# A decoder block on one core: GpSimd adds up one probability tile in four, ScalarE takes some of VectorE's copies, key splits are spread

## The chip, the cores and the metric

The kernel runs on one core of a Trainium2 chip. The metric is the device time of one execution in microseconds; it is the median over runs.

The engines are called as the profile calls them: PE (TensorE, the matrix engine; PEld is its weight loading), DVE (VectorE), ACT (ScalarE), POOL (GpSimd), SP (SyncE, which here only issues transfers).

## What is computed

One layer of a decoder block over 2048 positions with 1024 channels. The change touches attention alone. It has three groups of eight heads of 64 channels; each group looks at keys with a stride (1, 4, 16), in blocks of 128 queries against the block before and the own block:

```python
s = jnp.einsum('brnqhd,brnkhd->brnhqk', qb, kw) * (Dh ** -0.5)
s = jnp.where(valid[None, None, :, None], s, NEG_INF)
m = jnp.max(s, axis=-1, keepdims=True)
p = jnp.exp(s - m)
l = jnp.sum(p, axis=-1, keepdims=True)
o = jnp.einsum('brnhqk,brnkhd->brnqhd', p, vw)
```

Later `o / l` of the three groups are mixed with weights from `m + log(l)`. So each row of `p` needs its sum `l`, but nothing in attention itself waits for `l`: it is stored, and read after attention.

## The kernel before

The kernel has three stages. The input projection (up to 1443.7 us of the profiled span) is a long row of matrix products. Attention follows, to about 1645 us. Then come the output products.

Attention is written as 48 rounds, `i` from 0 to 47 (counted from 0 throughout this text; "rounds 9 to 40" of the change's short description, counted from 1, are `i` = 8 to 39). Four rounds make a unit: one group and one pair of heads. The groups take turns: rounds 0 to 3 are of group 0, 4 to 7 of group 2, 8 to 11 of group 1, 12 to 15 of group 0 again. A round has four query blocks `j`, each with two heads `h`. Where a block has no block of keys before it (all of group 2, the first round of a unit of group 1, one block in the first round of a unit of group 0) its rows are 128 wide, else 256. Twelve rounds (24 to 35, say) are one full turn of the pattern.

The order of the instructions on each engine is the order of the code; nothing moves them. In round `i` the code does this:

- `scores(i)`: PE makes the scores in four PSUM tiles (`s`), 24 products.
- `peak(i, j, h)`: DVE adds the mask, writes the tile `p` and takes the row's extreme into `sta` (L1015).
- `expo(i, j, h)`: ACT takes the exponential of `p` in place; with `accum_out` it also sums each row into `sta` (L1023). The sum is fetched by an instruction of its own, ACTIVATION_READ_ACCUMULATOR.
- `turn(i-1, w)`: PE transposes the pair `w` of tiles `p` of the round before into PSUM (`pt`, L1034).
- `bring(i, w, k, eng)`: DVE (L1049) or ACT (L1047) copies one half of that to SBUF (`ptb`).
- `values(i-2)`: PE multiplies with the values into `o` (L1064), and `leave(i-3)` copies `o` out on DVE (L1073 to L1079).

Three of the four copies of a round have fixed engines. The fourth, `bring(i-2, 1, 0, ...)`, goes to DVE when `light` holds, else to ACT.

A tile `p` lives in a pool of eight buffers, so the tile of round `i` is written again by `peak` of round `i+2`.

POOL splits each unit's keys into a high and a low part, in four quarters, each a CAST (L809) and a TENSOR_TENSOR (L811) on the tile `B` of the unit. The keys of unit `u` are loaded in round `4u-8` and used from round `4u` on. `later(lag, fn)` puts `fn` at the start of the round that is `lag` rounds on.

Of the kernel before, what the change touches and what calls it, by code (L numbers as in the profile page):

```python
# [8 lines left out]
F32 = mybir.dt.float32  # L9
F32R = mybir.dt.float32r  # L10
AF = mybir.ActivationFunctionType
ALU = mybir.AluOpType
# [3 lines left out]
P = 128  # L16
# [4 lines left out]
CH = 512  # L21
# [10 lines left out]
def hybrid_block_kernel(ctx: ExitStack, tc: tile.TileContext, a: dict, out: bass.AP):  # L32
    nc = tc.nc
    sp, act, dve, pool, pe = nc.sync, nc.scalar, nc.vector, nc.gpsimd, nc.tensor

    def flat(t):
        return t.bitcast(F32)
# [24 lines left out]
    cst = ctx.enter_context(tc.tile_pool(name="cst", bufs=1))  # L62
# [15 lines left out]
    act.dma_start(lr, a["lru_vec"])  # L78
    brh = cst.tile([P, 2, 8], F32, name="brh")
    HALF = (slice(0, 64), slice(64, P))  # L80
    gr_free = [cst.tile([P, P], F32, name=f"gr{j}") for j in range(2)]
    sp2 = cst.tile([P, 8], F32, name="sp2")


# [2 lines left out]
    def big(slot, shape, dt, name):  # L87
        return (Y if slot[0] == "Y" else Z if slot[0] == "Z" else X).tile(shape, dt, name=name, tag=slot)
# [5 lines left out]
    def later(lag, fn):  # L94
        late.append((now["n"] + lag, fn))
# [4 lines left out]
    def run(queue):  # L100
        due = [x for x in queue if x[0] <= now["n"]]
        queue[:] = [x for x in queue if x[0] > now["n"]]
        for _, fn in due:
            fn()
# [443 lines left out]
    light = [("v", FT_V + 2 * j, FT_V + 2 * j + 1) for j in range(6)]  # L548
# [157 lines left out]
    for s, pl in enumerate(plan):  # L706
        if pl[4] == "ug" and not (pl[0] and pl[1][1][0] - FT_U in put_off):
            at(base[s] + 1, lambda i=pl[1][1][0] - FT_U: fetch_gr(i))
        if pl[0] and pl[4] == "ug":
            i = pl[1][1][0] - FT_U  # L710
# [38 lines left out]
    def bring(t, b, c):  # L749

        at(t - 3, lambda: [keep_raw(b, c, kk) for kk in K4])
        at(t, lambda: [one_block(b, kk) for kk in K4])
# [36 lines left out]
    def unit(u):  # L789

        return (0, 2, 1)[u % 3], u // 3

    def unit_parts(u):

        qs, ks = USLOT[u % 3]
        g, hp = unit(u)
        q = {n: qk_scr[n, 4 * g + hp] for n in ("qh", "ql", "k")}
        units[u] = [None, None]

        def k_part(j):  # L800
            cols = slice(j * S // 2, (j + 1) * S // 2)

            def split(t):
                K = units[u][1]
                if u == 0:
                    act.activation(K[:, 0, t], flat(K[:, 1, t]), AF.Copy)
                    eng = dve
                else:
                    pool.tensor_copy(K[:, 0, t], flat(K[:, 1, t]))  # L809
                    eng = pool  # L810
                eng.tensor_tensor(out=K[:, 1, t], in0=flat(K[:, 1, t]), in1=flat(K[:, 0, t]), op=ALU.subtract)  # L811

            def fn():
                if j == 0:
                    units[u][1] = big(ks, [P, 2, S], F32R, f"B{u}")
                sp.dma_start(flat(units[u][1][:, 1, cols]), q["k"][:, cols])
                for i in range(2):
                    c0 = (2 * j + i) * CH
                    later(3 + i if u < 2 else 1, lambda c0=c0: split(slice(c0, c0 + CH)))
            return fn  # L820

        def q_part(i, n):
            def fn():
                if i == 0:
                    units[u][0] = big(qs, [P, 2, S], F32R, f"A{u}")
                sp.dma_start(flat(units[u][0][:, i]), q[n])
            return fn

        return [k_part(0), k_part(1), q_part(0, "qh"), q_part(1, "ql")]
# [3 lines left out]
    def v_parts(g, j):  # L833
        src = v_scr[g][j]

        def part(i):
            def fn():
                if i == 0:
                    VT[g, j] = big(VSLOT[g, j], [P, 16, 256], F32, f"V{g}{j}")
                V = VT[g, j]  # L840
                if g == 0:
                    sp.dma_start(V[:, 4 * i:4 * i + 4], src[i * CH:(i + 1) * CH].rearrange("(n p) f -> p n f", p=P))
                elif g == 1:
                    sp.dma_start(V[:, 4 * i:4 * i + 4], src[i * CH:(i + 1) * CH].rearrange("(j r) f -> j r f", r=4))
                else:
                    sp.dma_start(V[:, 4 * i:4 * i + 4], src.rearrange("(i r) f -> i r f", r=16)[:, 4 * i:4 * i + 4])
            return fn

        return [part(i) for i in range(4)]
# [74 lines left out]
    first, second, third, firstv = unit_parts(0), unit_parts(1), unit_parts(2), v_parts(0, 0)  # L924
# [20 lines left out]
    n = len(where)  # L945
# [16 lines left out]
    at_p = stB.enter_context(tc.tile_pool(name="at_p", bufs=2, reuse_waits="tile"))  # L962
# [3 lines left out]
    def prev(g, n):  # L966
        if g == 0:
            return n - 1 if n >= 1 else None
        if g == 1:
            return n - 4 if n >= 4 else None  # L970
        return None

    st = {}

    sta, stg, ot = {}, {}, {}

    def first(i, j):
        u, q = divmod(i, 4)
        g, _ = unit(u)
        return 0 if prev(g, 4 * q + j) is not None else P  # L980
# [29 lines left out]
    def peak(i, j, h):  # L1010
        u, q = divmod(i, 4)
        lo = first(i, j)
        if h == 0:
            st["p", i, j] = p_p.tile([P, 2, 256], F32, tag="p", name=f"p{i}{j}")
        dve.tensor_tensor_reduce(out=st["p", i, j][:, h, lo:256], in0=st["s", i, j // 2][h][:, j % 2, lo:256],  # L1015
                                 in1=mask[:, lo:256], scale=1.0, scalar=3e38, op0=ALU.add, op1=ALU.min,
                                 accum_out=sta[u][:, 4 * q + j, h:h + 1])

    def expo(i, j, h):
        u, q = divmod(i, 4)  # L1020
        p = st["p", i, j][:, h, first(i, j):256]
        s = sta[u][:, 4 * q + j]
        act.activation(p, p, AF.Exp, scale=-1.0, bias=s[:, h:h + 1], accum_out=s[:, 2 + h:3 + h])  # L1023

    def turn(i, w):
        js = (2 * w, 2 * w + 1)
        pp = [st.pop(("p", i, j)) for j in js]
        tag = "s" if (i, w) == (NG - 1, 1) else "t"
        t = st["t", i, w] = [aps.tile([P, 2, 2, 2, 64], F32, tag=tag, name=f"pt{i}{w}{k}", bufs=4) for k in range(2)]
        for j in js:  # L1030
            for x in range(first(i, j) // P, 2):
                for h in range(2):
                    for k, r in enumerate(HALF):
                        pe.transpose(t[k][:, j % 2, x, h, :], pp[j % 2][r, h, x * P:(x + 1) * P], ident[r, r])  # L1034
# [61 lines left out]
    def split(h, l, eng=dve):  # L1096

        r = flat(l)
        if eng is pool:
            pool.tensor_copy(h, r)  # L1100
        else:
            act.activation(h, r, AF.Copy)
        eng.tensor_tensor(out=l, in0=r, in1=flat(h), op=ALU.subtract)
# [22 lines left out]
    for i in range(NG):  # L1126
        u = i // 4
        turns, copied = i > 0, i > 1
        run(late)
        if i in VORD:  # L1130
            loads += v_parts(*VORD[i])
        if i % 4 == 0 and 1 <= u <= 9:
            loads += unit_parts(u + 2)
        for _ in range(2):
            if loads:
                loads.pop(0)()
        light = copied and (unit((i - 2) // 4)[0] == 2 or i % 3 == 1 or i == 2)
        scores(i)
        if i > 2 and ("o", i - 3) in st:
            leave(i - 3)  # L1140
        if copied:
            bring(i - 2, 1, 1, dve)
            if light:
                bring(i - 2, 1, 0, dve)
        if turns:
            expo(i - 1, 2, 1)
        if copied and not light:
            bring(i - 2, 1, 0, act)
        if turns:
            expo(i - 1, 3, 0)  # L1150
            expo(i - 1, 3, 1)
        peak(i, 0, 0)
        expo(i, 0, 0)
        for j, h in ((0, 1), (1, 0), (1, 1)):
            peak(i, j, h)
        if turns:
            turn(i - 1, 0)
            more = i in (1, NG - 1) or i % 4 == 0 and unit(u)[0] == 2
            bring(i - 1, 0, 0, dve if more else act)
            bring(i - 1, 0, 1, dve)  # L1160
        for j, h in ((0, 1), (1, 0), (1, 1)):
            expo(i, j, h)
        if copied:
            values(i - 2)
            if i == NG - 1:
                leave(i - 2, True)
        peak(i, 2, 0)
        peak(i, 2, 1)
        if turns:
            turn(i - 1, 1)  # L1170
        peak(i, 3, 0)
        peak(i, 3, 1)
        expo(i, 2, 0)
        if i in (40, 41):
            prep_wl(i - 40, 2)
        if 42 <= i < 46:
            load_h(0, 2 * (i - 42), 2)
            load_h(0, 2 * (i - 42) + 1, 2)
        if i in (46, 47):
            prep_wl(i - 44, 2)  # L1180
        now["n"] += 1
# [179 lines left out]
    for n in range(32):  # L1361
        c, f = divmod(n, 8)
# [229 lines left out]
```

## Time and profile before

| What | us |
|---|---|
| median of three runs (2103.78 to 2104.52) | 2103.8 |
| the profiled execution's own time | 2103.62 |
| its span, from the first to the last instruction | 2101.9 |
| attention, from the first score to 1640 | 196.3 |

About 1.7 us of the profiled execution lie outside its span. Read the profile by stage: PE is busy 99% of the whole span, but attention is a stage of its own, and there four engines matter. A row of a timeline gives start, duration, engine, line, operation, output and inputs. Durations of neighbours on one engine overlap, so what one instruction costs its engine is the distance from its start to the next start.

### The profile page before, as it was taken

The page shows a single profiled execution, that of the slowest core. Times are in us where ns is not written, and L with a number is a line of the kernel's source. Part 1 is how long each engine was busy: PE and PEld are TensorE (multiplying, and loading weights), DVE is VectorE, ACT ScalarE, POOL GpSimd, SP SyncE. Part 2 cuts the span into 40 slices and gives each one's busy share as a digit, 9 for nine tenths or more (in the row PEclk, how much of TensorE's full clock was granted, in tenths as well). Part 3 has the DMA queues.
Part 4 walks back from the last instruction along what each step waited for, and adds up shares of the span by engine and source line. Part 5 has one row for each costly group of instructions (what it writes and reads, how often), then busy time and mean ns, then how long its engine had stood idle before and what let it go on. Part 6 is the DMA issues. An engine that isn't in the chain of part 4 may idle for free.

```text
span 2101.9 us, 35814 instructions
## 1 busy us (share of the span) xinstructions
PE 2086.3 (99%) x12016; PEld 1726.9 (82%) x12016; DVE 1662.7 (79%) x3179; ACT 1116.7 (53%) x2341; POOL 493.1 (23%) x468
## 2 busy tenths in 40 slices
PE   8999999999999999999999999999999999999998
PEld 7888888888888888888888888888999888888887
DVE  8987888889988867787877888877999645576667
ACT  6455456457457565666666775766999411211100
POOL 1111111110111011231221222222545344431120
PEclk9999999999999999999999999999999999999999
DMA  8987997987997967777779778769996788864432
GB/s 271 276 261 225 274 285 216 282 283 235 278 294 242 332 208 204 231 227 220 225 254 278 254 252 266 252 219 374 355 359 236 228 296 281 298 224 160 154 105 71
DMA packets 327160, 524.69 MB, mean 250 GB/s; under 512 B 105536, under 2 KB 135232, under 8 KB 323136
## 3 DMA queue, kind: packets, MB, share of 16 engines
q1 hardware_dynamic: 307088, 489.54, 70.5%
q0 software_dynamic: 12256, 19.42, 5.5%
q10 hardware_dynamic: 7632, 13.44, 1.7%
q8 instruction: 96, 1.57, 0.3%
q14 instruction: 88, 0.72, 0.1%
HBM read 317.14 MB, written 190.45 MB: 241 GB/s over the span
## 4 chain that ended last, share of the span: by engine, by line
PE 91%; DVE 3%; DMA 3%; ACT 2%; issue 1%; SPq 0%; DVEq 0%; ACTq 0%
PE q L622 66%; PE yb L1340 3%; PE yb L1341 3%; PE z L1451 3%; PE yb L1342 3%; PE z L1450 3%; PE z L1452 3%; ACT p L1023 2%; DVE p L1015 2%; PE ya L1419 1%; PE ya L1418 1%; PE ya L1420 1%; PE g L492 1%; PE vtp L358 1%; DMA B<-k_scr 1%; DMA o_scr<-ot 1%
## 5 line engine op out<-in xcount | busy, mean ns | idle before, releaser
L622 PE MATMUL q<-xT,hS 128*128 128x512 f32 x1680 | 521.0, 391 | 0.0
L622 PE MATMUL q<-xT,l 128*128 128x512 f32 x1120 | 436.0, 389 | 0.0
L622 PE MATMUL q<-xB,hA 128*128 128x512 f32 x1248 | 388.9, 393 | 6.0 <-ACT xB L215 6.0
L622 PEld LDWEIGHTS q<-xT,hS 128*128 128x128 f32 x1680 | 312.9, 188 | 69.0 <-issue 5.5
L622 PE MATMUL q<-xB,l 128*128 128x512 f32 x904 | 352.9, 390 | 0.0
L622 PEld LDWEIGHTS q<-xB,hA 128*128 128x128 f32 x1248 | 233.8, 189 | 57.3 <-ACT xB L215 6.0
L622 PEld LDWEIGHTS q<-xT,l 128*128 128x128 f32 x1120 | 210.2, 188 | 44.1
L622 PEld LDWEIGHTS q<-xB,l 128*128 128x128 f32 x904 | 170.3, 188 | 36.0
L245 POOL DMA_DIRECT2D wS<-in_w_in_dram x70 | 61.9, 950 | 491.5 <-DMA wS<-in_w_in_dram 140.0
L622 PE MATMUL q<-xB,hS 128*128 128x512 f32 x560 | 174.0, 392 | 0.0
L1023 ACT ACTIVATE p<-p,sta 128x256 f32<-128x256 f32 (+1 forms) x384 | 172.7, 469 | 1.2 <-PE pt L1034 0.8
L622 PE MATMUL q<-xT,hA 128*128 128x512 f32 x560 | 173.0, 390 | 0.0
L269 ACT ACTIVATE hA<-wA 128x512 fp32r<-128x512 f32 x218 | 134.9, 623 | 54.4 <-DMA wA<-in_w_in_dram 24.9
L269 ACT ACTIVATE hS<-S 128x512 fp32r<-128x512 f32 x175 | 109.0, 623 | 79.3 <-DVE S L227 49.0
L227 POOL TENSOR_TENSOR S<-S,wA 128x512 f32<-128x512 f32 x35 | 45.5, 1301 | 391.8 <-DVE S L227 208.8
L622 PEld LDWEIGHTS q<-xT,hA 128*128 128x128 f32 x560 | 104.7, 188 | 23.0 <-issue 1.5
L622 PEld LDWEIGHTS q<-xB,hS 128*128 128x128 f32 x560 | 104.0, 188 | 22.4 <-issue 1.5
L1015 DVE CUSTOM_DVE_ANT_0 p<-s,mask 128x256 f32<-128x256 f32 (+1 forms) x384 | 116.4, 360 | 0.2 <-PE s L1008 0.2
L1451 PE MATMUL z<-wo,mh 128*128 128x512 f32 (+1 forms) x264 | 101.0, 383 | 0.0
L1452 PE MATMUL z<-wo,ml 128*128 128x512 f32 (+1 forms) x264 | 101.0, 383 | 0.0
L1450 PE MATMUL z<-wo,mh 128*128 128x512 f32 (+1 forms) x264 | 101.0, 383 | 0.0
L227 DVE TENSOR_TENSOR l<-wA,hA 128x512 fp32r<-128x512 f32 x113 | 79.3, 702 | 26.9 <-ACT hA L269 26.6
(204 smaller groups left out, 4257.0 us busy)
## 6 DMA issues: line engine op xcount, KB each, us to landing
wA<-in_w_in_dram SPq DMA_DIRECT2D x253, 256.0 KB, 4.7
wl_scr<-l SPq DMA_DIRECT2D x105, 512.0 KB, 5.2
l<-wl_scr SPq DMA_DIRECT2D x105, 512.0 KB, 4.6
sw<-y SPq DMA_DIRECT2D x384, 64.0 KB, 3.2
wS<-in_w_in_dram SPq DMA_DIRECT2D x70, 256.0 KB, 4.8
wS<-in_w_in_dram POOLq DMA_DIRECT2D x70, 256.0 KB, 6.3
qh_scr<-hi SPq DMA_DIRECT2D x48, 256.0 KB, 5.5
v_scr<-vs SPq DMA_DIRECT2D x48, 256.0 KB, 4.4
```

Of the source, the lines that this page charges most:

```text
L227: eng.tensor_tensor(out=out, in0=in0, in1=in1, op=op)
L245: pool.dma_start(t, w_part(s, x), accum_op=ALU.add)
L269: act.activation(h, r, AF.Copy)
L622: pe.matmul(bank, w[:, ks], x[:, kk, xx], start=(first and i == 0), stop=(last and i == 11))
L1015: dve.tensor_tensor_reduce(out=st["p", i, j][:, h, lo:256], in0=st["s", i, j // 2][h][:, j % 2, lo:256], in1=mask[:, lo:256], scale=1.0, s ...
L1023: act.activation(p, p, AF.Exp, scale=-1.0, bias=s[:, h:h + 1], accum_out=s[:, 2 + h:3 + h])
L1340: pe.matmul(yb, WL[f][:, 0, k], xx[:, 0], start=(k == 0), stop=False)
L1341: pe.matmul(yb, WL[f][:, 0, k], xx[:, 1], start=False, stop=False)
L1342: pe.matmul(yb, WL[f][:, 1, k], xx[:, 0], start=False, stop=(k == 7))
L1450: pe.matmul(z, mh[:, k], w[:, 0, hs], start=(k == 0), stop=False)
L1451: pe.matmul(z, mh[:, k], w[:, 1, hs], start=False, stop=False)
L1452: pe.matmul(z, ml[:, k], w[:, 0, hs], start=False, stop=(k == 7))
```

## The change

It has three parts. First, in rounds 8 to 39 the tiles of `j` = 0 are exponentiated without `accum_out`, and POOL adds up their rows (`add_up`): it folds a tile of two heads in halves, 128, 64, 32, 16 and 8 wide (from 64 where the rows are 128 wide), and once in four rounds it adds the last eight of all four rounds and writes the sums. Second, `light` no longer holds for the rounds with `i % 3 == 1` from 9 to 40, unless the copied round is of group 2; in rounds 10, 13, 16, 22, 25, 28, 34, 37 and 40 that copy goes from DVE to ACT. Third, the quarters of the keys of units 4 to 10 are split 3, 4, 5 and 6 rounds after their load instead of one round after it; unit 11 keeps one round. The two small tiles `gr` become one, `grt`, since attention uses it for the folds.

```diff
-    gr_free = [cst.tile([P, P], F32, name=f"gr{j}") for j in range(2)]
+    grt = cst.tile([P, 2, P], F32, name="grt")
+    gr_free = [grt[:, j] for j in range(2)]
...
-                    later(3 + i if u < 2 else 1, lambda c0=c0: split(slice(c0, c0 + CH)))
+                    later(3 + i if u < 2 else 3 + 2 * j + i if 4 <= u < 11 else 1, lambda c0=c0: split(slice(c0, c0 + CH)))
...
-        act.activation(p, p, AF.Exp, scale=-1.0, bias=s[:, h:h + 1], accum_out=s[:, 2 + h:3 + h])
+        if j or not 8 <= i < 40:
+            act.activation(p, p, AF.Exp, scale=-1.0, bias=s[:, h:h + 1], accum_out=s[:, 2 + h:3 + h])
+            return
+        act.activation(p, p, AF.Exp, scale=-1.0, bias=s[:, h:h + 1])
+        if h:
+            add_up(i)
+
+    fold_t = grt
+    rest_t = at_p.tile([P, 4, 2, 8], F32, name="rest_t", bufs=1)
+
+    def add_up(i):
+        u, q = divmod(i, 4)
+        src = st["p", i, 0][:, :, first(i, 0):256]
+        n = (256 - first(i, 0)) // 2
+        while n >= 8:
+            dst = rest_t[:, q] if n == 8 else fold_t[:, :, 0:n]
+            pool.tensor_tensor(out=dst, in0=src[:, :, 0:n], in1=src[:, :, n:2 * n], op=ALU.add)
+            src, n = dst, n // 2
+        if q < 3:
+            return
+        while n > 1:
+            pool.tensor_tensor(out=rest_t[..., 0:n], in0=rest_t[..., 0:n], in1=rest_t[..., n:2 * n], op=ALU.add)
+            n //= 2
+        sums = sta[u].rearrange("p (q j) f -> p q j f", j=4)[:, :, 0, 2:4]
+        pool.tensor_tensor(out=sums, in0=rest_t[..., 0], in1=rest_t[..., 1], op=ALU.add)
...
-        light = copied and (unit((i - 2) // 4)[0] == 2 or i % 3 == 1 or i == 2)
+        light = copied and (unit((i - 2) // 4)[0] == 2 or i == 2 or i % 3 == 1 and not 9 <= i < 41)
```

In the order of the instructions the numbers in a name tell the place: `p250` is the tile of round 25, `j` = 0, and `B10` holds the keys of unit 10. On POOL, the keys of units 10 and 11 stood alone before:

```order
L809 CAST B10_17662<-B10_17662 128x512
L811 TENSOR_TENSOR B10_17662<-B10_17662 128x512
L809 CAST B11_18055<-B11_18055 128x512
L811 TENSOR_TENSOR B11_18055<-B11_18055 128x512
L809 CAST B11_18055<-B11_18055 128x512
```

Now the folds of round 36 and 37 stand around them (the last rows of unit 11's four quarters, and what follows):

```order
L810 CAST B11_18199<-B11_18199 128x512
L812 TENSOR_TENSOR B11_18199<-B11_18199 128x512
L1040 TENSOR_TENSOR grt_201<-p370_18364 128x256
L1040 TENSOR_TENSOR grt_201<-grt_201 128x2x64
L1040 TENSOR_TENSOR grt_201<-grt_201 128x2x32
L1040 TENSOR_TENSOR grt_201<-grt_201 128x2x16
L1040 TENSOR_TENSOR rest_t_14442<-grt_201 128x16
L810 CAST B10_17784<-B10_17784 128x512
L812 TENSOR_TENSOR B10_17784<-B10_17784 128x512
```

What moved: the fold of `p370` waits in POOL's row behind the third quarter of `B10` and all four quarters of `B11`, and the last quarter of `B10` waits behind that fold.

On DVE, the start of round 25 before (a copy out, two copies of `pt`, then the peaks):

```order
L1077 COPY ot5_16431<-o22_16896 128x512
L1049 COPY ptb231_16979<-pt2311_16917 128x8x64
L1049 COPY ptb231_16979<-pt2310_16916 128x8x64
L1015 ISA p250_16985,sta0_14454<-s2500_16950,mask_185 128x256
L1015 ISA sta0_14454 128x1
```

and on ACT now, with the exponentials around it:

```order
L1025 ACTIVATE p242_16998,sta0_14454<-p242_16998,sta0_14454 128x256 x2
L1072 ACTIVATE ptb231_17058<-pt2310_17001 128x8x64
L1025 ACTIVATE p243_17019,sta0_14454<-p243_17019,sta0_14454 128x256 x2
L1027 ACTIVATE p250_17064<-p250_17064,sta0_14454 128x256
L1072 ACTIVATE ptb240_17085<-pt2400_17071 128x6x64
```

What moved: the copy of `pt2310` left DVE's row, so the peaks of round 25 follow one copy earlier, and it stands on ACT between two pairs of exponentials of round 24. The exponentials of `p250` no longer write `sta`.

## The prediction

> **What bounds the kernel now.** First the page: the chain of work that ended last is PE for 91% of the span, so elsewhere little is to be gained. Rounds are counted from 0.
>
> ```profile
> PE 91%; DVE 3%; DMA 3%; ACT 2%; issue 1%; SPq 0%; DVEq 0%; ACTq 0%
> ```
>
> The 3% of DVE and 2% of ACT lie in attention. So next the busy times there (span, PE, PEld, DVE, ACT, POOL), and the starts of the scores of rounds 24 and 36:
>
> ```profile
> 1443.70:1640.00 196.30, 194.24 (x3458) 176.31 (x3457) 195.99 (x936) 194.25 (x821) 106.52 (x116) 1.00 0.87 321
> ```
> ```profile
> 1540.45 0.54 PE L1008 MATMUL s<-B,A 64*128 64x128 f32 x6
> 1590.10 0.53 PE L1008 MATMUL s<-B,A 64*128 64x128 f32 x6
> ```
>
> PE, DVE and ACT are all full; POOL has 90 us free. Which of three full engines sets the pace? The groups by shape give the pieces (busy, mean ns, idle before), a timeline gives distances:
>
> ```profile
> L1023 ACT ACTIVATE p<-p,sta 128x256 f32<-128x256 f32 x212 | 105.8, 524 | 0.0
> L1023 ACT ACTIVATION_READ_ACCUMULATOR p<-p,sta 128x1 f32 x380 | 79.2, 208 | 0.0
> L1015 DVE CUSTOM_DVE_ANT_0 p<-s,mask 128x256 f32<-128x256 f32 x214 | 77.5, 418 | 0.0
> L1049 DVE COPY ptb<-pt 128x512 f32<-128x512 f32 x62 | 41.2, 683 | 0.0
> L1015 DVE CUSTOM_DVE_ANT_0 p<-s,mask 128x128 f32<-128x128 f32 x168 | 38.5, 285 | 0.2 <-PE s L1008 0.2
> L1049 DVE COPY ptb<-pt 128x256 f32<-128x256 f32 x60 | 23.3, 416 | 0.0
> L1047 ACT ACTIVATE ptb<-pt 128x512 f32<-128x512 f32 x36 | 21.6, 601 | 0.0
> L1047 ACT ACTIVATE ptb<-pt 128x256 f32<-128x256 f32 x20 | 7.4, 368 | 0.0
> L384 ACT ACTIVATE y<-y,bh 128x512 f32<-128x512 f32 x1 | 0.7, 725 | 2.0 <-DVE y L227 2.0
> ```
> ```profile
> 1550.93 0.68 DVE L1049 COPY ptb<-pt 128x512 f32<-128x512 f32 x1
> 1551.53 0.41 DVE L1015 CUSTOM_DVE_ANT_0 p<-s,mask 128x256 f32<-128x256 f32 x1
> ...
> 1552.78 0.23 ACT L1023 ACTIVATION_READ_ACCUMULATOR p<-p,sta 128x1 f32 x1
> 1552.88 0.62 ACT L1047 ACTIVATE ptb<-pt 128x512 f32<-128x512 f32 x1
> ...
> 1553.36 0.54 ACT L1023 ACTIVATE p<-p,sta 128x256 f32<-128x256 f32 x1
> ...
> 1553.75 0.24 ACT L1023 ACTIVATION_READ_ACCUMULATOR p<-p,sta 128x1 f32 x1
> ```
>
> On DVE a 512-wide copy costs 0.60 (1550.93 to 1551.53). A duration overlaps the next start by 0.075 to 0.083, so a peak costs 0.343 or 0.21, a 256-wide copy 0.333. On ACT the 512-wide copy costs 0.48, a summing exponential 0.39 and its fetch 0.10 (0.09 to 0.10 by the rows). Rounds 24 to 35 hold for DVE 54 peaks of 256, 42 of 128, 12 copies out, 16 copies of 512, one of 384 (0.47) and 15 of 256: 18.5 + 8.8 + 7.2 + 9.6 + 0.5 + 5.0 = 49.6. They last 49.65. DVE has no gap at all; it sets the pace. ACT, by the same count (54 exponentials at 0.49, 42 at 0.385, copies 6.5), has 49.2. PE comes third, with waits of its own:
>
> ```profile
> PEld s L1008 <- DVE sta L1015: 5.0, 23, 0.4
> PEld pt L1034 <- ACT p L1023: 4.0, 22, 0.4
> POOL B L809 <- DMA B<-k_scr: 56.8, 8, 13.6
> ```
>
> The chain of waits inside the stage shows where each rules: ACT back to back in rounds of group 2, PE back to back in rounds 24 to 28, DVE in most others.
>
> ```profile
> 1516.78 3.08 ACT p L1023 x16
> ...
> 1540.64 1.51 PE s L1008 x24
> 1542.14 0.49 PE pt L1034 x16
> 1542.63 1.93 PE o L1064 x32
> 1544.57 0.64 PE pt L1034 x16
> ...
> 1588.80 0.60 DVE ptb L1049
> ```
>
> **The copies.** Nine leave DVE: six of 512 and three of 256, 6 x 0.60 + 3 x 0.333 = 4.6 us. That is the most DVE can give. ACT takes them for 6 x 0.48 + 3 x 0.26 = 3.7 (368 ns less the overlap of about 0.1 for the latter).
>
> **The sums.** 64 fetches go, 64 x 0.093 = 6.0 us of ACT. Whether the exponential itself gets shorter no row shows. At best it would cost what a copy of its width does, 0.26 instead of 0.39; against that, an activation with a bias from memory takes 725 ns where a copy takes 601 at the same width, and a bias from memory is what the exponential has too. I take no saving beyond the fetch.
>
> **What DVE and ACT give together.** Per twelve rounds DVE falls to 49.6 - 1.5 = 48.1 and ACT to 49.2 - 2.2 + 1.2 = 48.2: ACT is now as full as DVE, and 49.65 can fall by at most 1.4. Nor do both fall evenly. Adding PE's pieces without the waits in them (1.51 + 0.49 + 1.93 + 0.64 for a full round, less in narrow ones), rounds 24 to 29 need 26.1 of PE against 25.1 of DVE and 25.5 of ACT; rounds 30 to 35 need 23.1 of DVE against 20.4 of PE. The worst of each half adds to 49.2, a gain of 0.45; if the four score tiles let one half lend all its slack to the other, the gain is 1.4. I take the middle, 0.9 per twelve rounds. The nine copies are three such turns: **-2.6 us**, between -1.3 and -4.6.
>
> **The folds on POOL.** No row has this operation; prices come from four pieces:
>
> ```profile
> 1563.63 0.61 POOL L809 CAST B<-B 128x512 fp32r<-128x512 f32 x1 [9.33 <-PE pt L1034]
> 1564.32 1.28 POOL L811 TENSOR_TENSOR B<-B 128x512 fp32r<-128x512 f32 x1
> 1565.55 0.60 POOL L809 CAST B<-B 128x512 fp32r<-128x512 f32 x1
> ...
> 2096.07 0.19 POOL L1478 TENSOR_TENSOR mv<-mv,epst 128x1 f32<-128x1 f32 x1 [17.45 <-DVE mv L1469]
> 2096.34 0.89 POOL L1479 TENSOR_TENSOR mv<-mv 128x1 f32<-128x1 f32 x1
> ```
> ```profile
> L1477 POOL MEMSET mv<- 128x1 f32 x1 | 0.1, 98 | 23.0 <-DVE x L1493 23.0
> ```
>
> An addition of one element takes 189 ns, one of 512 1284: 0.189 + 2.145 ns per element. An instruction that reads what the one before wrote starts 0.08 after its end; one that does not starts 0.05 before it. A quarter's split costs 1.92. A fold from 256 wide has 256, 128, 64, 32 and 16 elements: 5 x 0.189 + 1.06 + 4 x 0.08 - 0.05 = 2.28; from 128 wide 1.46; the last three additions 0.93. Below, 0.098 (a MEMSET reads nothing) bounds the base; above, nothing does but the full distance 0.27 of the last two rows, and I take 0.189, the same operation.
>
> Per twelve rounds POOL then has 6 x 2.28 + 6 x 1.46 + 3 x 0.93 + 12 x 1.92 = 48.3, against 49.65 - 0.9 = 48.8 available. It is hidden, barely, with two rounds of reserve in the eight buffers of `p`. The spread of the splits costs nothing in itself: POOL's wait of 56.8 us for keys (waits above) ends before each split is reached, and a unit's keys are ready two rounds before use. The exception is the end.
>
> ```profile
> 1558.25 0.55 ACT L1023 ACTIVATE p<-p,sta 128x256 f32<-128x256 f32 x1
> ```
> ```profile
> 1591.97 0.61 POOL L809 CAST B<-B 128x512 fp32r<-128x512 f32 x1 [8.20 <-DMA B<-k_scr]
> ```
> ```profile
> 1605.73 0.41 DVE L1015 CUSTOM_DVE_ANT_0 p<-s,mask 128x256 f32<-128x256 f32 x1
> ```
> ```profile
> 1608.56 0.30 PE L1008 MATMUL s<-B,A 64*128 64x128 f32 x1
> ```
>
> In round 37 stands the third quarter of `B10` and, loaded only one round before, all of `B11` (landed at 1591.97 before the change, so no wait for it). The tile of round 27 is ready at 1558.8 - 1.4 (five of nine copies gone) = 1557.4. From there POOL has the folds of 27 to 36 (20.7) and nine quarters (17.3): 1595.4. Five quarters more, 9.6: 1605.0. The first addition of the fold of round 37, 0.74: 1605.7. Only then may DVE overwrite that tile, in the first peak of round 39, which it would reach at 1605.73 - 2.3 = 1603.4: **+2.3 us**. The rest of that fold (1.5) and the last quarter of `B10` (1.9) end at 1609.1; the scores of round 40 need it and would start at 1608.56 - 2.3 + 2.3 = 1608.6: **+0.5**. Folds of rounds 38 and 39 hide under rounds 40 and 41. SP's store of `sta` after round 39 now waits for POOL; what is behind it are loads for rounds later.
>
> **Sum:** -2.6 + 2.3 + 0.5 = +0.2 on the profiled execution's 2103.62, which is itself 0.2 under the median of 2103.8. I predict 2103.8, no change: what a measurement of this kernel can tell is about 0.2%, 4.2 us.
>
> **A rule against the change.** The Trainium skill, "GPSIMD Engine Reference", Engine selection, sends elementwise additions to VectorE and calls GpSimd about half as fast; section 3.1 has 4497 ns for 2048 elements. With the row of 512 elements that gives an estimate of 0.214 + 2.09 ns per element, 0.02 more per small addition: about +1 on the sum, 2104.8.
>
> **Rivals.** *POOL becomes the bound (slower).* The place is its row of folds and splits from round 16 on, with 53 additions between rounds 27 and 36 and some 120 from round 15. Each 0.01 on the base of 0.189 is 0.5 us if the queue empties once at round 27, 1.2 if it never does. From +0.05, a base of 0.24, it passes 4.2 us; at 0.27 it is about +8, 2112. For it: two-row operands of 8 or 16 elements are in no row. Against: 0.189 is the same operation.
>
> *The jam at round 37 is small.* With a base of 0.10 the 53 additions are 4.7 us shorter, POOL waits for ACT instead, and both terms together shrink to 0.5: 2101.5. Faster than 2099.6 needs all of the 4.6 and almost no jam.
>
> *POOL and DVE share a port (slower).*
>
> ```profile
> L811 POOL TENSOR_TENSOR B<-B x44: 1273/1284/1302, 1442.9 to 1598.4; 128x512 fp32r<-128x512 f32 x44
> ```
> ```profile
> L227 POOL TENSOR_TENSOR sw<-sw,sin x48: 1285/1571/2027, 778.8 to 1411.6; 128x512 f32<-128x512 f32 x48
> ```
>
> Additions in attention hardly vary, so DVE's work there does not disturb them; in the projection the same shape takes up to 2027. If the folds were slowed like the latter's median, 1.22 times, 47 us of folds from round 15 on grow by 10, less a reserve of 2: 2112. The Trainium skill, "Perfetto Trace Analysis", Optimizing Scalar/DVE Operations, warns of this shared port. The 44 rows do not show it here.
>
> **Chances.** Forecast (relief and jam about cancel) 0.62; small jam 0.20, of it 0.06 faster by over 0.2%; POOL the bound 0.14; port 0.04. So faster 0.06, same 0.76, slower 0.18. The range goes down to the small jam with somewhat more relief, 2100.6, and up to a base of 0.24 or a little more, 2108.4.
>
> **What would show it.** Right: L1023's fetches fall by 64; DVE shows idle time of about 2 us before the first peak of round 39, released by POOL; PE waits for POOL before the scores of round 40; small additions near 0.19 plus 0.002 per element. Wrong: additions of 16 elements over 0.28 with DVE waiting for POOL in many rounds, or DVE without any wait for POOL and attention shorter by 3 us or more.

## The result and the profile after

The changed kernel takes 2107.15 us (median of 22 runs, 2105.06 to 2109.64), the one before 2104.14 (22 runs, 2103.26 to 2105.03): a ratio of 1.0014, 95% interval 1.0008 to 1.0021, that is 1.7 to 4.4 us slower. The profiled execution took 2105.99, 2.37 more than that of before. The forecast was 2103.8, no change; the time lies in its range, but the way there was not the one forecast.

The changed kernel's page gives the chain of work that ended last, by engine:

```profile
PE 91%; ACT 4%; POOL 3%; DMA 1%; DVE 1%; issue 1%; DVEq 0%; ACTq 0%; SPq 0%; POOLq 0%
```

POOL, in no place of this chain before, now holds 3% of the span, and DVE 1% instead of 3%. Next the waits inside attention (engine and line, what it waited for, us in total, times, longest):

```profile
POOL B L810 <- DMA B<-k_scr: 43.8, 3, 24.4
...
DVE p L1016 <- POOL grt L1040: 3.8, 2, 1.9
...
POOL grt L1040 <- ACT p L1027: 1.5, 3, 0.5
...
PEld s L1009 <- POOL B L812: 1.1, 1, 1.1
```

DVE waits for POOL just twice, 1.9 us each time. One such wait was forecast. A timeline of DVE names both places, the first peak of round 10 and that of round 39:

```profile
1485.55 0.42 DVE L1016 CUSTOM_DVE_ANT_0 p<-s,mask 128x256 f32<-128x256 f32 x1 [1.92 <-POOL grt L1040]
```
```profile
1607.93 0.42 DVE L1016 CUSTOM_DVE_ANT_0 p<-s,mask 128x256 f32<-128x256 f32 x1 [1.90 <-POOL grt L1040]
```

POOL's timeline shows what it did ahead of the first. Four key quarters of unit 3 run from 1477.39 to 1485.06; the fold of round 8, whose tile the peak of round 10 overwrites, stands behind them:

```profile
1477.39 0.61 POOL L810 CAST B<-B 128x512 fp32r<-128x512 f32 x1 [5.50 <-DMA B<-k_scr]
1478.08 1.30 POOL L812 TENSOR_TENSOR B<-B 128x512 fp32r<-128x512 f32 x1
...
1483.15 0.60 POOL L810 CAST B<-B 128x512 fp32r<-128x512 f32 x1
1483.83 1.27 POOL L812 TENSOR_TENSOR B<-B 128x512 fp32r<-128x512 f32 x1
1485.06 0.45 POOL L1040 TENSOR_TENSOR grt<-p 128x128 f32<-128x128 f32 x1
```

Its first addition ends at 1485.51 and the peak starts at 1485.55. In the kernel before, the same quarters stood nearly at the same time (first and last row), and DVE reached this peak before the last one ended:

```profile
1476.96 0.61 POOL L809 CAST B<-B 128x512 fp32r<-128x512 f32 x1 [5.69 <-DMA B<-k_scr]
...
1483.42 1.28 POOL L811 TENSOR_TENSOR B<-B 128x512 fp32r<-128x512 f32 x1
```
```profile
1483.49 0.41 DVE L1015 CUSTOM_DVE_ANT_0 p<-s,mask 128x256 f32<-128x256 f32 x1
```

Ahead of the second wait stand the third quarter of `B10` and four of `B11`, as forecast, and the scores of round 40 then wait for the last quarter of `B10` (POOL, then PE):

```profile
1597.55 0.61 POOL L810 CAST B<-B 128x512 fp32r<-128x512 f32 x1
...
1607.17 0.73 POOL L1040 TENSOR_TENSOR grt<-p 128x256 f32<-128x256 f32 x1
```
```profile
1611.41 1.34 PE L1009 MATMUL s<-B,A 64*128 64x128 f32 x20 [0.91 <-POOL B L812]
```

The groups by shape give the prices (busy, mean ns of one, idle before):

```profile
L1025 ACT ACTIVATION_READ_ACCUMULATOR p<-p,sta 128x1 f32 x316 | 64.1, 203 | 0.0
L1027 ACT ACTIVATE p<-p,sta 128x256 f32<-128x256 f32 x36 | 18.4, 512 | 2.6 <-DVE sta L1016 2.3
L1040 POOL TENSOR_TENSOR grt<-p 128x256 f32<-128x256 f32 x18 | 13.2, 735 | 1.9 <-ACT p L1027 1.5
L1040 POOL TENSOR_TENSOR grt<-grt 128x32 f32<-128x32 f32 x32 | 8.1, 252 | 2.5
L1040 POOL TENSOR_TENSOR rest_t<-grt 128x16 f32<-128x16 f32 x32 | 7.1, 221 | 2.5
```

By 0.189 us + 2.145 ns per element, additions of 256, 32 and 16 elements were to take 738, 258 and 223 ns. The 64 fetches are gone (380 to 316), and an exponential without sums (L1027) takes 512 ns, hardly less than the 524 of all before.

The stage's length is read from the first and last start of the scores (duration min/median/max, first to last start): 192.9 us before, 194.9 after.

```profile
L1008 PE MATMUL s<-B,A x1152: 268/277/385, 1443.7 to 1636.6; 64*128 64x256 f32 x108, 64*128 64x128 f32 x84
```
```profile
L1009 PE MATMUL s<-B,A x1152: 269/277/384, 1444.1 to 1639.0; 64*128 64x256 f32 x108, 64*128 64x128 f32 x84
```

The table below follows the lateness through the stage, with the kernels of the experiments (next section) beside the changed one. It is worked out from one timeline of each: the start of DVE's first peak of a round (r10 is round 10), counted from the first scores of round 0, minus the same in the kernel before. Up to round 9 all kernels agree to 0.02. Later, kernels with the same code up to a round agree there to 0.03, unless they have the wait at round 10, whose size varies from run to run (+1.66 and +1.12 in the rows "changed" and "unit 11 spread"). What follows the last scores takes 465.0 in each. So hundredths can be read that the scatter of whole runs would hide.

| kernel | r10 | r18 | r24 | r30 | r36 | r38 | r42 | r47 |
|---|---|---|---|---|---|---|---|---|
| changed | +1.66 | +1.25 | +0.92 | +0.76 | +0.43 | -0.17 | +1.98 | +1.98 |
| folds from round 12 | -0.34 | +0.17 | -0.16 | -0.30 | -0.64 | -1.23 | +0.93 | +0.93 |
| unit 11 spread | +1.12 | +0.71 | +0.38 | +0.22 | -0.11 | -0.71 | -0.24 | -0.24 |
| both jams out | -0.32 | +0.20 | -0.13 | -0.29 | -0.62 | -1.21 | -0.77 | -0.77 |
| no additions | -0.34 | -0.47 | -0.80 | -0.95 | -1.28 | -1.88 | -1.43 | -1.43 |
| copies alone | -0.34 | +0.94 | +0.61 | +1.83 | +1.50 | +1.31 | +2.75 | +2.75 |
| additions alone | -0.01 | +0.02 | +0.02 | +0.04 | +0.04 | +0.04 | +0.07 | +0.07 |
| unit 3 after folds | -0.34 | -0.49 | -0.82 | -0.98 | -1.31 | -1.91 | -1.46 | -1.46 |
| three copies back | -0.33 | -0.78 | -1.11 | -1.57 | -1.90 | -2.50 | -2.36 | -2.36 |
| third bunch | -0.32 | -0.46 | +5.69 | +5.53 | +5.20 | +4.60 | +5.06 | +5.06 |
| extra addition | -0.32 | +1.36 | +3.17 | +4.55 | +6.34 | +6.42 | +6.53 | +6.53 |

For the changed kernel: two jumps, at round 10 and between rounds 38 and 42, and between them a slow fall. Of the 2.37 us of the profiled executions 1.98 are in this stage; the other 0.39 is a later start of round 0 (1444.09 against 1443.70), which lies between 1443.6 and 1445.2 in the traces of this study, all with the same code ahead of it.

### The profile page after: what moved, and what is told of

Its sections match the earlier page's. It is cut to its first block, busy times and chain, and to the rows that moved or that the text cites. A ratio compares the mean times of both kernels' runs of the same rounds, so it can differ in the third digit from the quotient of the medians.

```text
span 2104.3 us, 35929 instructions
## 1 busy us (share of the span) xinstructions
PE 2084.2 (99%) x12016; PEld 1725.6 (82%) x12016; DVE 1659.6 (79%) x3170; ACT 1115.5 (53%) x2286; POOL 550.3 (26%) x638
## 3 DMA queue, kind: packets, MB, share of 16 engines
q8 instruction: 96, 1.57, 0.3%
## 4 chain that ended last, share of the span: by engine, by line
PE 91%; ACT 4%; POOL 3%; DMA 1%; DVE 1%; issue 1%; DVEq 0%; ACTq 0%; SPq 0%; POOLq 0%
PE q L623 66%; PE yb L1365 3%; PE yb L1366 3%; ACT p L1025 3%; PE z L1476 3%; PE yb L1367 3%; PE z L1475 3%; PE z L1477 3%; PE ya L1444 1%; PE ya L1443 1%; PE ya L1445 1%; PE g L493 1%; POOL B L812 1%; PE vtp L359 1%; PE o L1089 1%; POOL grt L1040 1%
## 5 line engine op out<-in xcount | busy, mean ns | idle before, releaser
L1025 ACT ACTIVATE p<-p,sta 128x256 f32<-128x256 f32 (+1 forms) x320 | 144.1, 463 | 0.9 <-DVE sta L1016 0.8
L623 PEld LDWEIGHTS q<-xT,hA 128*128 128x128 f32 x560 | 104.7, 188 | 23.1 <-issue 1.5
```

The lines of the kernel that those rows point to most:

```text
L623: pe.matmul(bank, w[:, ks], x[:, kk, xx], start=(first and i == 0), stop=(last and i == 11))
```

## Experiments

Call it a jam when a fold stands in POOL's row behind a bunch of key quarters and DVE has to wait for it. The theory to be tested (A): two jams, at round 10 and at round 39, make the time, and nothing else in the change costs anything. Against it B: every addition costs something, by POOL's load or by a port; and C: the copies on ACT cost it.

**Folds from round 12 on.** No fold stands behind unit 3's quarters.

```diff
-        if j or not 8 <= i < 40:
+        if j or not 12 <= i < 40:
```

> Folds in rounds 12 to 39 only, so that in POOL's row no fold stands behind unit 3's four key quarters, which land at 1477.39. Theory A (two jams in POOL's row, about 2.0 us at round 10 and about 2.1 at rounds 39 and 40, made the time, against a relief of about 1.5): the first peak of round 10 no longer waits for a fold, and the time falls by 2.0 to about 2105.2. Theory B (the additions cost something in every round, by POOL or by a port that it shares with DVE): 22 additions of 170 fewer give 22/170 of about 4.5 us, so about 2106.6. Theory C (the copies moved to ACT cost it): nothing here touches them, 2107.2.

2105.33 (ratio 1.0007, 0.9998 to 1.0016). The jump at round 10 is gone (-0.34 for +1.66). The end gains 1.05, not 2.0, because rounds 8 to 11 have their fetches again while ACT already takes a copy there: +0.51 from round 10 to 18, where the changed kernel falls by 0.41. The same folds make 0.69 at round 18 between two kernels without a jam ("both jams out" +0.20, "unit 3 after folds" -0.49).

**Unit 11 spread.**

```diff
-... 3 + 2 * j + i if 4 <= u < 11 else 1
+... 3 + 2 * j + i if 4 <= u < 12 else 1
```

> Unit 11's key splits are spread over rounds 39 to 42 as those of units 4 to 10 are, so that the fold of round 37 stands behind one key quarter and not five. Theory A: the shift that the trace shows from round 38 (+0.22) to round 42 (+2.37) goes, and the time falls by about 2.1 to about 2105.0; the first jam stays at 2.0. Theories B and C: no addition and no copy is changed, so about 2107.2.

2104.0 (1.0001, 0.9992 to 1.001). The second jump is gone, the end 2.2 earlier; 0.5 of that is a smaller first jam in this trace (+1.12 for +1.66).

**Both edits.** Folds from round 12 on, and unit 11 spread.

> Both edits at once: folds in rounds 12 to 39 and unit 11's splits spread. Theory A: both jams go, about 4.1 less than the changed kernel, near 2103.0, that is about 1 below the kernel before; no wait of DVE for POOL above 0.3 us is left in rounds 8 to 42. Theory B: about 2106.6. Theory C: 2107.2.

2103.45 (0.9997, 0.9988 to 1.0006), and DVE waits for POOL nowhere. Against the run with folds from round 12 this prices the second jam without the scatter of the first: 0.93 + 0.77 = 1.70.

**No additions.**

```diff
-        if h:
-            add_up(i)
...
```

> No additions at all: the first exponentials of rounds 8 to 39 give no sums and POOL adds none up (these sums are left out of the result and stand at 1); copies and splits as in the changed kernel. It shows what ACT and DVE gain where POOL's part costs nothing. Theory A: as the run without the two jams, within 0.5, so 2102.5 to 2103.3. Theory B: clearly below that run, by 1.5 us or more, since every addition's cost is gone. Theory C: still above the kernel before, 2104.1 or more.

This kernel leaves out the sums of those tiles; a constant stands in their place. 2103.23 (0.9996, 0.9987 to 1.0004), its scores ending 1.43 earlier than before the change. From round 24 to 36 it falls by 0.48, the changed kernel by 0.49. So the additions cost nothing between the jams, and B is out. At round 18 the changed kernel stands 1.72 (1.25 + 0.47) above this one, at round 10 it was 2.00: that is the first jam less what was regained.

**Copies alone.** All exponentials sum as before, no additions.

```diff
-        if j or not 8 <= i < 40:
+        if True:
```

> Every exponential gives its sums again and POOL adds nothing; the nine copies stay on ACT and the splits where the change puts them. Theory A (the relief is that of ACT's 64 fetches, which pay for the copies that ACT takes over): without them ACT ends last over most of rounds 10 to 41, nothing is gained, and the scores end 1.5 to 3.5 us later than in the run without additions, so about 2105.5 to 2107. Rival: the fetches were hidden on ACT anyway, and then this takes as long as the run without additions, about 2103.2.

2107.03 (1.0013, 1.0004 to 1.0022). A table by stretch (us, then busy time and instructions of PE, PEld, DVE, ACT, POOL, and last the granted clock, the DMA engines' share and GB/s; this run first, then the kernel before) shows ACT with no gap and DVE with 1.5 us of them; before the change it was DVE that had none:

```profile
1487.50:1541.70 54.20, 52.16 (x956) 47.75 (x956) 52.73 (x249) 54.20 (x225) 28.62 (x31) 1.00 0.90 344
```
```profile
1487.50:1541.70 54.20, 53.97 (x980) 49.45 (x979) 54.20 (x257) 53.92 (x225) 28.57 (x31) 1.00 0.93 355
```

ACT's fetches were not hidden: while they stay, the same nine copies cost 2.75 instead of gaining 1.43.

**Additions alone.** Both jams out, the nine copies on DVE.

```diff
-... i % 3 == 1 and not 9 <= i < 41)
+... i % 3 == 1)
```

> Folds in rounds 12 to 39 and both jams out, with the copies as in the kernel before (nine on DVE again). Theory A: DVE ends last in most of these rounds as before, ACT's shorter exponentials only lengthen its waits, and the time is that of the kernel before within 0.4: about 2104.4. Rival: the exponentials' relief alone carries the gain of the run with both jams out, about 2103.4; a second rival, that the additions cost DVE or the rounds something of their own: 2105 or more.

2104.8 (1.0002, 0.9993 to 1.0011); in the table +0.07 at most. A faster ACT alone buys nothing while DVE has no gap.

**Unit 3 after folds.** All folds and copies of the change; unit 3's quarters in rounds 10 to 13, unit 11's spread.

```diff
-... 3 + 2 * j + i if 4 <= u < 11 else 1
+... 3 + 2 * j + i if 4 <= u < 12 else 6 + 2 * j + i if u == 3 else 1
```

> The changed kernel with all its folds and copies, and two schedules changed: unit 3's key quarters are split in rounds 10 to 13, each behind a fold, and unit 11's are spread. Theory A: both jams go while the relief of rounds 8 to 11 stays, so the time is that of the run without any addition, within 0.3: about 2103.0, its scores ending 1.4 earlier than in the kernel before. Theory B (additions cost something wherever they stand): 1 us or more above that run.

2102.67 (0.9994, 0.9985 to 1.0003). In the table it is the run without additions to 0.03 in every column. So all of the loss in the stage was in where the quarters stood. It is a narrow fit, though: the quarters that came later fill POOL's row, and the fold of round 20 now begins at 1532.42, its first addition ending 0.34 before the peak of round 22 (at 1533.22), which writes the same buffer; this time is called the fold's slack here:

```profile
1532.42 0.46 POOL L1040 TENSOR_TENSOR grt<-p 128x128 f32<-128x128 f32 x1
```

**Three copies back.** The run before this one, with the copies of rounds 16, 28 and 40 on DVE again:

```diff
-... i % 3 == 1 and not 9 <= i < 41)
+... i % 3 == 1 and (not 9 <= i < 41 or i % 12 == 4))
```

> As the run with unit 3's quarters behind the folds, and besides the copies of rounds 16, 28 and 40 are on DVE again, six being left on ACT. Theory A, with its reading of the trace that in rounds 16 to 17, 28 to 29 and 40 to 41 ACT ends last and DVE stands idle for about 0.7 to 1 us: each copy that goes back costs DVE 0.6 that it has, and saves ACT 0.9 there, so each twelve rounds gain 0.3 to 0.5 more and the time falls to 2101.8 to 2102.2, the fastest of all. Rival: DVE ends last there too, and the three copies cost 0.6 each: about 2104.8.

2102.22 (0.9989, 0.998 to 0.9998): the fastest, below both kernels, its interval just clear of no change. The reason is a stretch of eleven us around rounds 28 and 29 (columns as above), first with nine copies moved, then with six:

```profile
1559.00:1570.00 11.00, 10.76 (x208) 10.14 (x206) 10.31 (x56) 10.71 (x46) 9.90 (x21) 1.00 0.93 340
```
```profile
1559.00:1570.00 11.00, 11.00 (x212) 10.28 (x212) 10.96 (x58) 10.64 (x47) 9.90 (x21) 1.00 0.89 333
```

DVE's gap of 0.7 closes and PE has none left. In the run with nine, DVE waits 0.61 there for values; PE in turn, by the waits of that stretch, waited for a copy by ACT (DVE, then PE's weight loads):

```profile
1567.26 0.69 DVE L1100 COPY ot<-o 128x512 f32<-128x512 f32 x1 [0.61 <-PE o L1089]
```
```profile
PEld o L1089 <- ACT ptb L1072: 0.4, 1, 0.4
```

This kernel has even less room on POOL: its fold of round 20 has a slack of 0.04.

**A third bunch, made on purpose.** Unit 7's quarters back in one piece:

```diff
-... if 4 <= u < 12 else 6 + 2 * j + i if u == 3 else 1
+... if 4 <= u < 12 and u != 7 else 6 + 2 * j + i if u == 3 else 1
```

> The run with unit 3's quarters behind the folds, in which unit 7's four quarters are put back in a bunch before the fold of round 20, which is not in the change: a jam made on purpose, in a place where POOL does not wait for keys. Theory A (a fold that stands behind a bunch is late by the bunch, and the first peak two rounds on, which takes the same buffer, is late by that less the slack): in that run the fold of round 20 starts at 1532.42 and its first addition ends 0.34 before the peak of round 22 begins; four quarters of 1.92 put before it make that peak about 7.3 late, little of it is regained, and the time rises by 6.5 to 7.3, to about 2109.5. Theory B (a cost per addition): no addition is added, about 2102.7.

2109.95 (1.0028, 1.0018 to 1.0037), where 2109.5 was expected. One round was miscounted: the bunch lies before the fold of round 21, so the peak of round 23 waits:

```profile
1544.71 0.42 DVE L1016 CUSTOM_DVE_ANT_0 p<-s,mask 128x256 f32<-128x256 f32 x1 [6.39 <-POOL grt L1040]
```

In the run with unit 3 after folds that fold had a slack of 1.25 (its first addition ended at 1536.52, the peak came at 1537.77): 4 x 1.92 - 1.25 = 6.4. That is the rule of the jams in one line. The stage is 6.52 longer than in that run. That the time came near the expected one is in part luck, since it had been worked out from the slack of another fold, 0.34.

The trace shows one thing more. PE stood idle for 5.48 behind this wait, and from 1543.0 to 1549.9 its granted clock was about half, where it was 1.00 in the rest of attention:

```profile
1546.22 1.01 PE L1059 MATMUL pt<-ident,p 64*128 64x64 f32 x14 [5.48 <-ACT ptb L1072]
```
```profile
1543.00:1549.90 6.90, 3.68 (x44) 3.68 (x44) 5.19 (x24) 4.72 (x17) 6.27 (x12) 0.51 0.50 200
```

In that stretch 23 score products of 128 columns took 2.90, where 20 took 1.34 in the row of 1611.41 above. Over a whole execution the mean granted clock was 0.997 or 0.998 in all ten executions of this kernel.

**An extra addition.**

```diff
+            if n == 32:
+                pool.tensor_tensor(out=fold_t[:, :, 64:64 + n], in0=src[:, :, 0:n], in1=src[:, :, n:2 * n], op=ALU.add)
```

> The run with unit 3's quarters behind the folds, with one more addition of 64 elements per fold into an unused piece of the scratch tile: about 0.27 us of POOL a round. Theory A together with what that run's trace shows, namely that POOL never idles from round 11 to the end and that the slack of a fold falls from 6.2 at round 10 to 0.34 at round 20: ten more additions of 0.27 from round 11 to 20 make 2.7, the slack covers 0.3 of it, and the peak of round 22 comes about 2.4 late; from there the slack grows by more than 0.27 a round, so nothing is added later: about 2104.7 to 2105.1. Rival: POOL, which is busy for less than nine tenths of the time, has room, and the time stays at 2102.7. Theory B: 32 more additions at the rate of 170 for 4.5 us, 2103.5.

2110.99 (1.0033, 1.0021 to 1.0044): far over what I expected, for two reasons. The price was 0.40, not 0.27; the addition behind it, which does not need its result but overwrites half of what it reads, starts 0.08 after its end and not before it:

```profile
1520.52 0.32 POOL L1041 TENSOR_TENSOR grt<-grt 128x64 f32<-128x64 f32 x1
1520.92 0.65 POOL L1042 TENSOR_TENSOR grt<-grt 128x64 f32<-128x64 f32 x2
```

Counted from the first scores, POOL begins the fold of round 20 at 92.11 instead of 87.81, 4.30 later than without these additions (ten of them are 4.0); the slack there falls from 0.34 to 0.03, and the peak of round 22 is 3.98 later (+3.16 for -0.82). And the short rounds 30 to 33 did it again (from +2.66 at round 29 to +6.33 at round 34): where POOL has nothing to spare the slack that was used up did not come back in between. DVE waited for POOL eleven times:

```profile
DVE p L1016 <- POOL grt L1042: 6.2, 11, 1.1
```

**The changed kernel twice more.**

> The changed kernel once more, for a second trace of it: its runs lie between 2105.1 and 2109.6 and the one in the first trace was 2106.0. Theory A1: the first jam has no fixed size, since its start is the landing of unit 3's keys (1477.39 in the first trace) while the first peak of round 10 keeps its own time; a run above 2106.0 then shows a later landing against the stage's start and a longer wait of that peak, by the same amount. Theory A2: the jams are as in the first trace to 0.1 us, and the difference lies outside rounds 0 to 47.

> A third trace of the changed kernel, read as the second: by theory A1 the excess over 2106.0 is that of the landing of unit 3's keys, by theory A2 it lies outside rounds 0 to 47.

2106.57 and 2105.22. The first jam has no fixed size. Counted from the first scores of round 0, unit 3's first quarter starts 33.30 after them in the first trace, 32.69 and 32.20 in these, 32.73 in the run with unit 11 spread; the peak of round 10 then waits for 1.92, 1.34, 0.83 and 1.37. It is the same step, one for one. In two of the four the profile puts that quarter's start down to the key load, in the other two to a peak of DVE, so what sets it is not shown. But 2106.57 does not lie above 2105.99 for this reason: its jam was smaller, and round 0 began 1.1 later (1445.20). So A1 holds for the size of the jam and A2 for that run's excess.

## Why the prediction was right and wrong

- **The step that failed** is the sentence "The spread of the splits costs nothing in itself: POOL's wait of 56.8 us for keys (waits above) ends before each split is reached, and a unit's keys are ready two rounds before use. The exception is the end." There was a second exception, at the start. Unit 3 keeps the lag of one round, its keys come at 1477.39, and its four quarters stand in POOL's row ahead of the first fold. It was in the trace before: POOL's timeline there has the first quarter at 1476.96, after a wait of 5.69 for keys, and the last one ending at 1484.70, while the first peak of round 10 stands at 1483.49. I asked whether keys come in time for the scores that read them, and not what newly stands behind the instruction that waits. The jam cost 0.8 to 1.9 at round 10 in four traces; in the first it was worth 1.72 at round 18.
- **The relief was sized too high:** -2.6 forecast, -1.43 and -1.46 measured without jams. The reasoning gave 0.45 to 1.4 per twelve rounds, and I took the middle, 0.9 (three times that is 2.7, not 2.6); from round 24 to 36 it was 0.48, the lower end, as if the two halves did not lend each other slack (26.22 and 22.95 from first peak to first peak, against 26.1 and 23.1). But the reason given for the first half, that PE needs 26.1 there, does not hold: with six copies moved instead of nine the same rounds take 25.91. With nine, ACT holds one more copy in rounds 16, 28 and 40, PE waits for it, and DVE idles. With six the gain was 0.79 per twelve rounds and 2.36 in all: three of the nine made it smaller.
- **The jam at the end was right in place and mechanism:** DVE's wait before round 39 of 1.90 against +2.3, PE's wait for `B10` of 0.91 against +0.5. Together 2.15 from round 38 to 42; since the kernels without this jam also lose 0.45 there (-1.88 to -1.43 without additions), it is worth 1.70, as the pair of runs says, against the 2.8 forecast. POOL's row from the fold of round 27 to that of round 37 took 47.28 (1559.89 to 1607.17), against 47.6 forecast.
- **The sum by measured terms:** -1.45 + 1.72 + 1.70 = +1.97, against 1.98 in the stage. In the forecast, relief and jam were both about one too large and cancelled, which was luck; the missing jam is what shows.
- **What the sum leaves open:** the medians differ by 3.0, 1.0 more than the stage of this trace. This 1.0 goes with PE's mean granted clock, which the forecast left aside. Nine of the 22 executions of the changed kernel have 0.999, and their median is 2106.22, 2.08 above the kernel before; thirteen have 0.996 to 0.998, and a median of 2107.62. With one jam left (folds from round 12; unit 11 spread) four of 11 executions each lie below 0.999; of the 66 executions of the six kernels without a jam, one does. So the jams seem to lower the clock at times, as the third bunch did. Whether that makes these executions longer, or a longer first jam or a later round 0 in the same executions, is not shown: none of them was traced, and in the third bunch the stage grew by only 0.13 more than the wait.
- **Right:** the fetches alone are saved, and no more of the exponential; the prices of the additions, to 6 ns in the three sizes shown.
- **The rivals.** POOL as the bound did not come true here: the base stayed at 0.19, and in the changed kernel the folds outside the jams end 2.2 to 5.7 us before the peak that needs their tile, except the one behind each jam (0.03) and the fold of round 38 (0.44). It was near: with unit 3's quarters moved behind the folds the slack at round 20 is 0.34, and 0.40 more per round then cost 8.3 us. The shared port is out in this stage: the additions of the key splits take 1283 ns (1284 before), and the folds cost DVE at most 0.07. Nor was the jam small.

## What to carry to other kernels

When an in-order queue gets new work that someone waits for, walk that queue from its first new instruction to its last and ask of each what stands ahead, above all instructions that wait for a load; the lateness is the length of the bunch less the slack, and nearly all of it stays. A relief between two engines that are both full has to be worked out stretch by stretch, not as a mean over the stage; take the change in pieces, since a part of the moved work can be better left where it was. A queue that is busy for nine tenths can hide all of its work and yet have no room: its slack is the time from the end of its work to the instruction that needs it, and that is read from two timelines.

## What was not expected of the hardware

A pause of 5.48 us on PE came with half the granted clock for nearly 7 us (the third bunch), and executions of kernels with a jam have a lower mean clock more often than those without. In the three traces of the changed kernel, where PE's pauses in attention are at most 1.6, the clock stays at 1.00 there; how long a pause must be was not measured.

An addition on POOL that overwrites half of what the one before it reads starts 0.08 us after that one's end, like one that needs its result, so that an extra addition of 64 elements costs 0.40 us and not 0.27. Writing the same tile is not enough for that: the four quarters of a unit write one tile, and each starts 0.05 to 0.06 before the end of the one ahead (1478.89 against 1477.65 + 1.30 for unit 3 before the change).
